# Diffusion trunk on one core: first Strassen pair of each phase reordered, ctx z written in float32 by ScalarE, six modulation rounds from TensorE to VectorE

## Chip, cores and metric

The kernel runs on one core of a Trainium2 chip. The metric is the device time of one execution in microseconds (us); lower is better. The engines are TensorE (PE, its weight loads PEld), VectorE (DVE), ScalarE (ACT), GpSimd (POOL) and SyncE (SP), whose queue issues most DMAs.

## The reference, cut to what matters

A trunk of two layers over 256 latent and 256 context (ctx) tokens of width 1024. Each layer is a modulated half-step SwiGLU, a token mixer (gMLP and attention in layer 0, mLSTM in layer 1) and a second half-step SwiGLU. The modulation vectors come from one matrix per layer, 1024 x 9216, times two vectors (one for latent tokens, one for ctx).

```python
def modulate(z, g, shift, scale):
    return rmsnorm(z, g) * (1 + scale) + shift

def swiglu(z, w13, w2):
    gate, up = jnp.split(z @ w13, 2, axis=-1)
    return (jax.nn.silu(gate) * up) @ w2
...
    for l in range(DEPTH):
        m_l = (s_lat @ mod_w[l] + mod_b[l]).reshape(b, N_MOD, 1, d)
        m_c = (s_ctx @ mod_w[l] + mod_b[l]).reshape(1, N_MOD, 1, d)
        h = h + 0.5 * m_l[:, 2] * swiglu(modulate(h, norm_g[l, 0], m_l[:, 0], m_l[:, 1]), ffn_w13[l, 0], ffn_w2[l, 0])
```

## The kernel before

**Precision.** Every float32 operand is split into a high part (ScalarE's copy to float32r) and a low part (VectorE's difference); `mm3` makes three matmuls, high by high, high by low and low by high. `wsplit` (L104 to L110) does it for weights: L108 the high part, L109 the low part, with four buffers of each (`NWH`). Raw weights lie in four slots of 1 MB (`rawp`), which DMAs on SP's queue fill.

**Phases.** `ffn512` runs three times over all 512 tokens: phase 1 (layer 0, first SwiGLU), phase 2 (layer 0, second) and phase 3 (layer 1, first). The last SwiGLU is another function. A phase has 11 column groups `cc` of 256 gate and 256 up columns. Most are a Strassen pair: gate and up by latent and ctx is a 2 x 2 block product done in seven products of half size, each 24 matmuls of 256 columns. Their operands on the token side are B11, B21, B22 (quarters of z) and T1 to T4 (sums of quarters, made once in a phase by `combos_lat`, `combos_ctx`, `combos_last` from z in float32); on the weight side a1, a2, g2 (plain weights), S1, S3 (sums that an accumulating DMA on POOL's queue makes in memory, L761), S2 = S3 + g2 and S4 = S2 + a2 (sums by VectorE, L776 and L778, written over a1's raw weights). `pair_products` runs the products in the order a1 B11, S2 T2, S1 T1, S3 T3, a2 B21, g2 T4, S4 B22 on three PSUM banks a, b, c; `pr.split` ahead of a product splits its weights, and `nx` is the next pair, whose loads (`Pair`, `plain`) are issued one pair ahead. The first column group of phases 2 and 3 is done directly, latent half first, then the ctx half, while the ctx half of z is still being normalised (`norm_z`: L408 VectorE, L411 ScalarE high part, L412 VectorE low part; its statistics go through a power on POOL, L125, and small pieces of it are queued in `pend` and run by `poke` between matmuls). Phase 1 does column groups 0, 1 and 2 directly, as six tiles of 128 gate and 128 up columns: three in the prologue, three here with `whole_tile`. After six column groups, and again after the other five, w2's products follow in columns `dp` with blocks of four.

**Modulation rounds.** A round is 512 columns of a modulation matrix; layer 0's rounds 0 to 3 are done in the prologue, the others in one of two ways. `mod_direct` does two rounds on TensorE: 32 matmul records (L310), a copy by ScalarE, four transposes and a sum by VectorE. `mod_round_dve` does one on VectorE: sixteen multiply-adds of 512 elements (L263, L265; eight from round 10 of layer 1 on, where the ctx vector isn't needed), which accumulate, and at its end four one-hot matmuls (L275, eight records) that set the sums into a PSUM bank shared by a group of rounds (`GROUPS`); the last of a group copies, transposes and adds the bias. It is a generator: `fill` runs one step of it, two multiply-adds, and `tick` calls `fill` at a rate per block of w2 (`FILL`); `mvec` runs what is missing where a vector is needed. Steps are given a priority 60 instructions ahead (`LEAD`). `until` is the last round that may be started.

**Order.** A scheduler at compile time orders each engine's instructions by priority (the order in the code) and readiness in its own model; on the chip each engine and each DMA queue runs its list in order.

## Time and profile before

| | before |
|---|---|
| three runs, median | 1736.99 us |
| three runs, lowest and highest | 1734.05, 1737.80 us |
| profiled execution | 1733.01 us |
| its span | 1731.3 us |
| granted TensorE clock over the span | 0.989 of 2.4 GHz |

The profile is of one execution. A table of stretches gives the busy time of each engine and the granted clock: 1.00 is 2.4 GHz, and a mean below it tells how much of the stretch ran at 1.2 GHz. In order of time, a row is start, duration, engine, line, operation, out<-in, and in brackets the idle time of the engine before it and what ended it. Matmuls overlap: a row's duration is longer than the distance to the next start, and the distance counts.

### The profile page before, as it was taken

Reading aid. Unit: us, or ns where it says so; the run is one execution under the profiler, and the core shown is the slowest. Engines: PE = TensorE matmul, PEld = TensorE weight load, DVE = VectorE, ACT = ScalarE, POOL = GpSimd, SP = SyncE. Lnnn points to the kernel's source line nnn. Section 1 sums busy time; section 2 is a strip of 40 time slices with the busy share of each in tenths; the row PEclk is TensorE's granted clock in tenths of the full one; section 3 lists DMA queues with packets and bytes.
Section 4 is the critical chain, followed back from the end, with each engine's and each line's share of the span. In section 5 each row is a group of like instructions: output and inputs, shape, how many; then the busy total and the mean of one; then the engine's idle time right before and its main releaser. Section 6 shows DMA issues by size and latency. Waiting matters only on the chain.

```text
span 1731.3 us, 30536 instructions
## 1 busy us (share of the span) xinstructions
PE 1687.0 (97%) x12247; PEld 1522.2 (88%) x12247; DVE 1259.1 (73%) x2067; ACT 739.2 (43%) x1140; POOL 287.7 (17%) x333
## 2 busy tenths in 40 slices
PE   7999999999999989999999899999999999999998
PEld 5799699989877989979998899779988788899998
DVE  5768668758665688967877888677876986695554
ACT  4443235424654355413542455214533554364443
POOL 0130133004432034013300241023200001100000
PEclk9999999999999989999999999999999999999999
DMA  9785787353466278468734586688555563146552
GB/s 282 211 179 183 215 219 175 106 163 110 150 226 147 66 176 186 158 184 206 172 108 159 132 204 153 232 224 202 121 191 153 188 226 122 50 130 211 189 180 71
DMA packets 274881, 292.63 MB, mean 169 GB/s; under 512 B 14648, under 2 KB 240948, under 8 KB 274740
## 3 DMA queue, kind: packets, MB, share of 16 engines
q1 hardware_dynamic: 242452, 261.31, 47.2%
q0 software_dynamic: 32256, 29.37, 11.8%
q8 instruction: 96, 1.57, 0.4%
q14 instruction: 45, 0.37, 0.1%
q10 hardware_dynamic: 32, 0.01, 0.0%
HBM read 289.60 MB, written 1.05 MB: 168 GB/s over the span
## 4 chain that ended last, share of the span: by engine, by line
PE 79%; issue 11%; DVE 7%; ACT 1%; SPq 1%; DMA 1%; POOL 1%; DVEq 0%; POOLq 0%; ACTq 0%
PE pb L789 14%; PE ps L114 11%; PE ps L116 11%; PE ps L115 11%; PE pc L789 9%; PE pa L789 9%; PE ps L1004 2%; PE ps L1006 2%; PE ps L1005 2%; PE mdir_ps L310 1%; DVE wlo L109 1%; PE mod_ps L275 1%; DVE zlo L412 1%; DVE nt L408 1%; PE pv_ps L1340 1%
## 5 line engine op out<-in xcount | busy, mean ns | idle before, releaser
L108 ACT CAST whi<-raw 128x1024 fp32r<-128x1024 f32 (+2 forms) x208 | 211.1, 1017 | 352.1 <-PE ps L115 183.4
L109 DVE TENSOR_TENSOR wlo<-raw,whi 128x1024 fp32r<-128x1024 f32 (+2 forms) x208 | 244.2, 1182 | 114.3 <-ACT whi L108 113.9
L761 POOL DMA_DIRECT2D rsum<-in_ffn_w_dram x224 | 197.8, 1037 | 607.3 <-DMA rsum<-in_ffn_w_dram 316.4
L114 PE MATMUL ps<-hh,whi 128*128 128x512 f32 (+1 forms) x764 | 270.5, 354 | 2.5 <-ACT whi L108 2.5
L116 PE MATMUL ps<-hh,wlo 128*128 128x512 f32 (+1 forms) x764 | 268.1, 351 | 1.7 <-DVE wlo L109 1.7
L115 PE MATMUL ps<-hl,whi 128*128 128x512 f32 (+1 forms) x764 | 268.5, 351 | 0.0
L114 PE MATMUL ps<-zhi,whi 128*128 128x256 f32 (+2 forms) x720 | 221.2, 310 | 3.1 <-ACT zhi L411 1.8
L116 PE MATMUL ps<-zhi,wlo 128*128 128x256 f32 (+2 forms) x720 | 219.6, 308 | 3.4 <-DVE wlo L109 3.3
L115 PE MATMUL ps<-zlo,whi 128*128 128x256 f32 (+2 forms) x720 | 219.8, 307 | 0.0
L108 ACT CAST whi<-rpl 128x1024 fp32r<-128x1024 f32 x112 | 117.7, 1051 | 186.2 <-DVE rpl L776 54.6
L109 DVE TENSOR_TENSOR wlo<-rpl,whi 128x1024 fp32r<-128x1024 f32 x112 | 136.8, 1222 | 71.4 <-ACT whi L108 71.2
L114 PEld LDWEIGHTS ps<-hh,whi 128*128 128x128 f32 x764 | 143.9, 188 | 30.1 <-issue 4.5
L116 PEld LDWEIGHTS ps<-hh,wlo 128*128 128x128 f32 x764 | 144.2, 189 | 25.5 <-DVE wlo L109 2.5
L115 PEld LDWEIGHTS ps<-hl,whi 128*128 128x128 f32 x764 | 144.0, 188 | 22.0 <-issue 1.6
L265 DVE SCALAR_TENSOR_TENSOR mod_acc<-raw,s_st,mod_acc 128x512 f32<-128x512 f32 x224 | 158.4, 744 | 4.8 <-DMA raw<-in_mod_w_dram 4.2
L114 PEld LDWEIGHTS ps<-zhi,whi 128*128 128x128 f32 x720 | 136.4, 190 | 14.9 <-issue 3.0
L116 PEld LDWEIGHTS ps<-zhi,wlo 128*128 128x128 f32 x720 | 135.9, 190 | 11.4 <-DVE wlo L109 4.4
L115 PEld LDWEIGHTS ps<-zlo,whi 128*128 128x128 f32 x720 | 136.5, 190 | 6.8 <-issue 1.0
L789 PE MATMUL pa<-zhi,wlo 128*128 128x256 f32 x448 | 128.6, 287 | 6.6 <-DVE wlo L109 6.6
L789 PE MATMUL pa<-zhi,whi 128*128 128x256 f32 x448 | 127.8, 285 | 1.7 <-ACT whi L108 1.7
L789 PE MATMUL pa<-zlo,whi 128*128 128x256 f32 x448 | 127.6, 285 | 0.0
L789 PE MATMUL pc<-zlo,whi 128*128 128x256 f32 x448 | 126.5, 282 | 0.0
(367 smaller groups left out, 4120.6 us busy)
## 6 DMA issues: line engine op xcount, KB each, us to landing
raw<-in_mod_w_dram SPq DMA_DIRECT2D x64, 1024.0 KB
raw<-in_ffn_w_dram SPq DMA_DIRECT2D x32, 1024.0 KB
raw<-in_ffn_w_dram SPq DMA_DIRECT2D x62, 512.0 KB
rsum<-in_ffn_w_dram SPq DMA_DIRECT2D x56, 512.0 KB
rsum<-in_ffn_w_dram POOLq DMA_DIRECT2D x224, 128.0 KB, 4.4
rpl<-in_ffn_w_dram SPq DMA_DIRECT2D x56, 512.0 KB
ra<-in_ffn_w_dram SPq DMA_DIRECT2D x28, 512.0 KB
raw<-in_ml_w_in_dram SPq DMA_DIRECT2D x12, 1024.0 KB
```

The lines of the kernel that those rows point to most:

```text
L108: act.copy(hi, view)
L109: dve.tensor_tensor(lo, view, hi.bitcast(F32), op=ALU.subtract)
L114: pe.matmul(ps, ah, bh, start=start, stop=False)
L115: pe.matmul(ps, ah, bl, start=False, stop=False)
L116: pe.matmul(ps, al, bh, start=False, stop=stop)
L265: dve.scalar_tensor_tensor(acc[:, v], raw[:, k], s1, acc[:, v], op0=ALU.mult, op1=ALU.add)
L275: pe.matmul(ps[32 * j : 32 * (j + 1), :256], onehot[:, MAXG - 1 - m : MAXG + 31 - m], acc[:, v, hf * 256 : (hf + 1) * 256], start=(m == 0) ...
L761: pool.dma_start(out=self.raw[n][:, k : k + 1], in_=src(cc, *two)[:, k : k + 1], accum_op=ALU.add)
L789: pe.matmul(o, a[:, k, cs], b[:, k], start=fresh and j == 0 and k == 0 and n == 0, stop=j == 1 and k == 3 and n == 2, skip_group_check=True,)
L1004: pe.matmul(o, zh, wh[:, k % 4], start=(k == 0), stop=False)
L1005: pe.matmul(o, zh, wl[:, k % 4], start=False, stop=False)
L1006: pe.matmul(o, zl, wh[:, k % 4], start=False, stop=(k == KD - 1))
```

## The change

- `ffn512` in phase 1: column group 2 is no longer two whole tiles but a pair, so a pair more and two 1 MB loads fewer.
- The first pair of each phase runs `pair_first`: order a1 B11, S4 B22, a2 B21, S2 T2, S1 T1, S3 T3, g2 T4, with S1 T1 on a fourth bank, d. The splits of a1, S2, S4 and a2 are all written ahead of it, and T1's.
- In phases 2 and 3 the first pair's loads (`Pair`) are written ahead of the direct tile, `combos` and `plain` between its latent and ctx half. ctx z in float32 is written by ScalarE in `norm_z` (eight operations of 256 elements) and not by two sums on VectorE.
- Modulation: layer 0's rounds 10, 11, 16, 17 and layer 1's 4 and 5 go from `mod_direct` to `mod_round_dve`. The even mixer has two `mod_direct` and not four, phase 3 has none, phase 1 keeps its one. The fill rates rise, a step is run after each pair, and in the odd mixer the first eight steps have no fill (`FILLODD`). In layer 0 the groups are (6, 12) and (16, 18), in layer 1 (4, 6) is new.

```diff
-FILL = ((1.9, 1.5), (1.9, 1.5), (1.9, 1.5))
-GROUPS = (((6, 10),), ((0, 4), (6, 10), (10, 12), (12, 16), (16, 18)))
+FILL = ((2.4, 2.1, 1), (2.4, 2.1, 1), (2.4, 2.1, 1))
+GROUPS = (((6, 12), (16, 18)), ((0, 4), (4, 6), (6, 10), (10, 12), (12, 16), (16, 18)))
-MIXDIRECT = {1: (10, 11), 4: (12, 13), 7: (14, 15), 10: (16, 17)}
+MIXDIRECT = {4: (12, 13), 8: (14, 15)}
+FILLODD = range(9, 33)
...
             act.activation(z[0][:, k, sl], t, AF.Identity, bias=B[:, k, half : half + 1])
+            if half == 1 and zctx[0] is not None:
+                act.activation(zctx[0][:, k], t, AF.Identity, bias=B[:, k, half : half + 1])
...
+            def pair_first(pr, nx, f):
+                a, b, c, d = bank("pa"), bank("pb"), abank("pc"), abank("pd")
+                w = pr.w
+                product(a, w["a1"], "B11", True)
+                s1 = sil_tile("s1")
+                act.copy(s1, a)
+                product(c, w["S4"], "B22", True)
+                product(a, w["a2"], "B21", False)
+                pr.split("S1")
+                product(b, w["S2"], "T2", True)
+                dve.tensor_tensor(s1, s1, b, op=ALU.add)
+                pr.split("S3")
+                product(d, w["S1"], "T1", True)
+                if nx:
+                    nx.plain()
+                pr.split("g2")
+                product(b, w["S3"], "T3", True)
+                s7 = sil_tile("s7")
+                dve.tensor_tensor(s7, s1, b, op=ALU.add)
+                dve.tensor_tensor(s7, s7, d, op=ALU.add)
+                act.activation(s7, s7, AF.Silu, scale=-1.0)
+                if nx:
+                    nx.split("a1")
+                product(b, w["g2"], "T4", False)
...
                 whole_tile(3, *first[1], 1)
-                combos_lat()
-                combos_ctx()
-                rg, ru = load_cc(2)
-                cc = 3
+                cc = 2
+                for n, ts in (("zlat", lat), ("zctx", ctx)):
+                    z_sum(z_tile(n), n, ts)
                 pr = Pair(cc)
-                for j in range(2):
-                    whole_tile(4 + j, rg, ru, j)
-                combos_last()
                 pr.plain()
-                pr.split("a1")
+                for n in ("a1", "S2"):
+                    pr.split(n)
+                combos()
+                split_to(mov["T1"], zf["zlat"][:, 0:4])
+                for n in ("S4", "a2"):
+                    pr.split(n)
             else:
...
                 cc = 1
+                z_sum(z_tile("zlat"), "zlat", lat)
+                zctx[0] = z_tile("zctx")
+                pr = Pair(cc)
                 for n, ts in enumerate((lat, ctx)):
...
-                    if n == 0:
-                        combos_lat()
-                    else:
+                    if n == 1:
                         settle()
-                        combos_ctx()
-                        pr = Pair(cc)
+                        zctx[0] = None
+                        combos()
+                        pr.plain()
...
-                combos_last()
-                pr.plain()
-                pr.split("a1")
+                for n in ("a1", "S2", "S4", "a2"):
+                    pr.split(n)
+                split_to(mov["T1"], zf["zlat"][:, 0:4])
...
-                    pair_products(pr, nx, cc * 2 - f0)
+                    (pair_first if ahead.pop() else pair_products)(pr, nx, cc * 2 - f0)
+                    ahead.append(False)
+                    tick(rates[2])
...
-                fill(1)
+                ran[0] += 1
+                if ran[0] in FILLODD:
+                    fill(1)
...
-    filler.extend([(0, r) for r in range(6, 10)] + [(1, r) for r in range(18) if r not in (4, 5)])
+    filler.extend([(0, r) for r in range(6, 12)] + [(0, 16), (0, 17)] + [(1, r) for r in range(18)])
...
-    ffn512(1, 0, z, nxt, FILL[2], direct=(4, 5))
+    ffn512(1, 0, z, nxt, FILL[2])
```

## Rows read from the trace of the kernel before

**Rows 1.** The page, busy us, share of the span and instructions of each engine.

```profile
PE 1687.0 (97%) x12247; PEld 1522.2 (88%) x12247; DVE 1259.1 (73%) x2067; ACT 739.2 (43%) x1140; POOL 287.7 (17%) x333
```

**Rows 2.** Stretches: start:end, length, busy us (instructions) per engine, granted clock, DMA.

```profile
612.00:641.00 29.00, 24.40 (x169) 23.40 (x168) 24.26 (x25) 15.07 (x18) 9.65 (x12) 0.82 0.72 164
...
641.00:732.00 91.00, 91.00 (x759) 90.37 (x758) 78.43 (x94) 46.21 (x55) 20.68 (x24) 1.00 0.70 180
...
980.00:1014.00 34.00, 28.26 (x214) 27.55 (x213) 29.04 (x29) 16.78 (x20) 10.58 (x12) 0.90 0.77 189
...
1109.00:1130.00 21.00, 18.33 (x96) 11.91 (x95) 13.14 (x22) 4.79 (x5) 0.00 (x0) 0.92 0.71 233
...
1354.00:1376.00 22.00, 18.33 (x71) 13.33 (x71) 21.61 (x45) 9.01 (x11) 0.00 (x0) 0.92 0.38 125
```

**Rows 3.** TensorE in order of time, even mixer: start, us, engine, line, operation.

```profile
458.74 3.64 PE L310 MATMUL mdir_ps<-raw,s_st 128*32 128x512 f32 x32
...
463.11 0.66 PE L119 MATMUL mdirT_ps<-ident,mdir_sb 128*128 128x128 f32 x4
```

**Rows 4.** TensorE in order of time, phase 3's direct rounds.

```profile
1111.05 3.64 PE L310 MATMUL mdir_ps<-raw,s_st 128*32 128x512 f32 x32
...
1117.63 0.50 PE L114 MATMUL ps<-hh,whi 128*128 128x512 f32 x1 [1.55 <-ACT whi L108]
```

**Rows 5.** Groups of instructions by line: busy us, mean ns | idle before, releaser.

```profile
L265 DVE SCALAR_TENSOR_TENSOR mod_acc<-raw,s_st,mod_acc 128x512 f32<-128x512 f32 x224 | 158.4, 744 | 4.8 <-DMA raw<-in_mod_w_dram 4.2
...
L108 ACT CAST whi<-rpl 128x1024 fp32r<-128x1024 f32 x112 | 117.7, 1051 | 186.2 <-DVE rpl L776 54.6 <-PE pc L789 47.4 <-PE pb L789 46.3
...
L109 DVE TENSOR_TENSOR wlo<-rpl,whi 128x1024 fp32r<-128x1024 f32 x112 | 136.8, 1222 | 71.4 <-ACT whi L108 71.2
...
L825 DVE TENSOR_TENSOR s<-s,pb 128x512 f32<-128x512 f32 x28 | 19.2, 686 | 14.6 <-PE pb L789 14.6
```

**Rows 6.** TensorE in order of time, one-hot matmuls together and spread.

```profile
337.40 0.64 PE L275 MATMUL mod_ps<-mod_acc,onehot 128*32 128x256 f32 x8
337.97 0.50 PE L114 MATMUL ps<-hh,whi 128*128 128x512 f32 x1
...
767.67 0.39 PE L116 MATMUL ps<-hh,wlo 128*128 128x512 f32 x1
767.99 0.62 PE L275 MATMUL mod_ps<-mod_acc,onehot 128*32 128x256 f32 x2
...
771.79 0.40 PE L115 MATMUL ps<-hl,whi 128*128 128x512 f32 x1
```

**Rows 7.** SP queue, TensorE and VectorE in order of time, start of phase 1.

```profile
61.44 1.74 SPq L97 DMA_DIRECT2D raw<-in_ffn_w_dram  x2
...
66.95 0.50 PE L114 MATMUL ps<-zhi,whi 128*128 128x512 f32 x1 [0.74 <-ACT sil L847]
...
72.96 0.92 SPq L759 DMA_DIRECT2D rsum<-in_ffn_w_dram  x2
...
88.82 1.23 DVE L776 TENSOR_TENSOR rpl<-rsum,rpl 128x1024 f32<-128x1024 f32 x1 [2.73 <-DMA rsum<-in_ffn_w_dram]
```

**Rows 8.** Chain that ended last, in order of time: start, us, what.

```profile
100.64 2.88 PE pa L789 x24
...
120.50 2.88 PE pa L789 x24
```

**Rows 9.** TensorE in order of time, first product of phase 2.

```profile
623.59 0.39 PE L789 MATMUL pa<-zhi,wlo 128*128 128x256 f32 x1 [2.27 <-DVE wlo L109]
```

**Rows 10.** TensorE in order of time, odd mixer.

```profile
1358.28 0.50 PE L116 MATMUL ps<-zhi,wlo 128*128 128x512 f32 x1 [1.99 <-DVE wlo L109]
...
1371.61 0.50 PE L116 MATMUL ps<-zhi,wlo 128*128 128x512 f32 x1 [1.31 <-DVE wlo L109]
```

**Rows 11.** POOL in order of time, start of phase 2.

```profile
602.94 0.70 POOL L125 TENSOR_TENSOR rs<-rs,mhalf 128x2 f32<-128x2 f32 x1 [17.21 <-DMA rsum<-in_ffn_w_dram]
...
609.70 2.66 POOL L761 DMA_DIRECT2D rsum<-in_ffn_w_dram  x3 [2.61 <-issue]
```

More of the change, by code (lines that the diff above doesn't have):

```diff
@@ L419, in norm_z @@
             )
+    zctx = [None]
     def norm_A(A, l, i, ks):
@@ L662, in ffn @@
                         elif half == 0 and k0 == 0:
-                            while current[0] is not None or (until[0] == (0, 17) and filler and filler[0] <= until[0]):
+                            while current[0] is not None or (until[0] == (0, 11) and filler and filler[0] <= until[0]):
                                 fill(1, more=False)
@@ L842, in pair_products @@
                 store(f, 2, s7, ctx)
+            def pair_first(pr, nx, f):
[22 more added lines that the diff above has]
+                product(b, w["g2"], "T4", False)
+                s2 = sil_tile("s2")
+                dve.tensor_tensor(s2, s1, c, op=ALU.add)
+                dve.tensor_tensor(s2, s2, d, op=ALU.add)
+                dve.tensor_tensor(s7, s7, s2, op=ALU.mult)
+                store(f, 2, s7, ctx)
+                dve.tensor_tensor(s1, s1, b, op=ALU.add)
+                act.activation(s1, s1, AF.Silu, scale=-1.0)
+                dve.tensor_tensor(s1, s1, a, op=ALU.mult)
+                store(f, 2, s1, lat)
             def hidden(f, pg, pu):
@@ L896, in ffn512 @@
                         mm3(pss[a][:, ts], ws[a][0][:, k], ws[a][1][:, k], z[0][:, k, ts], z[1][:, k, ts], k == 0, k == KD - 1)
[L897 to L899 removed]
+                for n in ("a1", "S2", "S4", "a2"):
+                    pr.split(n)
+                split_to(mov["T1"], zf["zlat"][:, 0:4])
                 for j in range(2):
                     hidden(j, pss[2 * j], pss[2 * j + 1])
+            ahead = [True]
             gate = tmp.tile([P, KD, 2], F32, tag="gate", name="gate")
@@ L953, in ffn512 @@
                             elif half == 0 and k0 == 0:
-                                while current[0] is not None or (until[0] == (0, 17) and filler and filler[0] <= until[0]):
+                                while current[0] is not None or (until[0] == (0, 11) and filler and filler[0] <= until[0]):
                                     fill(1, more=False)
@@ L1727, in odd_mixer @@
         g = kvo()
+        ran = [0]
         def run(n):
```

25 lines of the change are left out of this document (10 added, 15 removed).

## The prediction

> **What bounds the kernel now.** I read the busy table first [rows 1]: TensorE is busy 1687.0 of 1731.3 us, VectorE 1259.1, so time is won where TensorE's instructions become fewer or where it stands still. The table of stretches [rows 2] then shows where the missing 44 us and the slow clock are. In the pairs of a phase (641 to 732) nothing is lost. At the start of phase 2 (612 to 641) TensorE is idle 4.6 us and the granted clock is 0.82, so the 1.2 GHz level held for 0.36 of 29 us; counted in matmuls, 169 at the 0.120 us that 641 to 732 gives (91.0 / 759) are 20.3 us, so 8.7 us are lost. At the start of phase 3 (980 to 1014) 214 matmuls are 25.7 of 34 us: 8.3 lost. Around the direct rounds of phase 3 (1109 to 1130) it idles 2.7 us, and at clock 0.92 about 3.4 us run at half rate, which costs 1.7. At the start of the odd mixer (1354 to 1376) 3.7 us idle and 1.8 of clock are lost. In the even mixer the direct rounds cost only their own TensorE time.
>
> **The sum's base.** The profiled execution took 1733.0 us (span 1731.3); the median of the three runs is 1737.0, 4.0 more. I add the terms to the first and move the result to the median.
>
> **Direct rounds removed.** In the even mixer a pair of rounds is 32 records in 3.64 us and four transposes in 0.66 [rows 3]; the tail of each group overlaps what follows, so 3.6 and 0.4 are taken from the products. Two of four such pairs go: **-8.0**. Their eight 1 MB loads leave SP's queue there and appear in the feed-forward phases. In phase 3 the removed pair takes 3.6 us (1111.05 on), the next product starts only at 1117.63 after a wait of 1.55 on ScalarE [rows 4]; with the 2.7 idle and 1.7 of clock of that stretch and 0.3 of transposes it is **-8.2**. Between -4 (its own time alone) and -9.
>
> **The same six rounds on VectorE.** Each is 16 operations at 744 ns [rows 5], 11.9 us, 71 in all. They lie in stretches where VectorE has room: 78.4 of 91 us in the pairs [rows 2]. But TensorE isn't rid of them: each round ends in four one-hot matmuls (eight records). Where they stand together they take 0.6 to 0.7 us (337.40 to 337.97); where the compiled order has them one by one between the 512-column matmuls, 767.67 to 771.79 holds four one-hot steps and five ordinary matmuls, 4.12 less 5 x 0.234, 2.95 us [rows 6]. The twelve rounds of this size now stand in both forms and in one with two pieces; I take 1.5 each, near the mean of the ten that can be read, and 0.5 for two more group ends: **+9.5**, between 4 and 18. So about three fifths of what the direct rounds cost come back.
>
> **Phase 1's two whole tiles become a pair.** From 66.95 [rows 7], after a wait of 0.74, to 100.64 [rows 8] three whole tiles run in 33.7 us, so two take 22.5, each 48 matmuls of 0.234; a pair of seven products runs from 100.64 to 120.50, 19.9 us [rows 8]: -2.6. But the cover goes as well. The pair's first product needs a1, the second S4 = (S3 + g2) + a2. S3 is summed in memory: base load issued at 72.96, the add that uses it starts at 88.82, 15.9 us later [rows 7]. The new pair's base can't start before tile 3's weights leave their slot, when now the next weights start, 61.44 [rows 7]; so S3 is there at 77.3. Behind it is a serial chain, since every sum is written over the weights that the step before it still reads: add 1.22, S2 high 1.05, S2 low 1.22, add 1.22, S4 high 1.05 and low 1.22 [rows 5, 7], 7.0 us, to 84.3. TensorE ends tile 3 at 78.2 and a1's product at 81.0: 2.9 us wait (the high part lets it start a little before). Between 0 and 6.
>
> **A new wait in every first pair.** In the new order T3's and T4's products stand next to each other on bank b; T4's adds onto what T3's left, and between them VectorE must read b. Today another product stands there and hides it. The read takes 0.69 us and starts behind a wait on TensorE in nearly all pairs (14.6 us over 28) [rows 5]: 0.8 us three times if VectorE is free, 2 each if it isn't. Phase 1: -2.6 + 2.9 + 0.8 = **+1.1**.
>
> **First pairs of phases 2 and 3.** Removed: two VectorE sums of 1.2 us for ctx z (ScalarE writes it now, eight operations that run beside), and products that need T2 and T1 come fourth and fifth. Added ahead: S2, S4 and a2 splits, queued on VectorE behind the combinations. Today the a1 product waits 2.27 us for its low part [rows 9]. Laid out with the rows' durations, a1's low part is there at about 620 in phase 2, as the direct tile ends; VectorE still has two further splits and the end of the combinations in its queue, and the chain of 7 us above ends near 628.5, where a1's product ends at 623. So TensorE stands 5.4 us before the second product instead of in three pieces before and in the first two. All later operands are then ready. With the bank's 0.8 the loss is 6.3 at full clock, and 1.6 more at 1.2 GHz: 7.9 against 8.7 and the 0.6 of smaller waits around, 9.3. In phase 3 the same layout gives 9.8 against 8.3 and 1.5 of waits up to the second pair: nothing won. **-1.4** for both. Bounds: a1's slot frees 4.3 us before the direct tile ends, so with VectorE free the chain would end 2.2 us late, and -7 each; with T4 and the hidden tiles served first, +3 each.
>
> The half rate stands in the rows where TensorE was busy 24.4 of 29 us, and a wait of the size of today's keeps its cost in my layout [rows 2]. The Trainium skill, "TensorE: Matmul & The Clock Gate", section on the HAM clock gate, makes half rate the default that activity releases, and lists it for an idle engine; read that way a first pair with scattered waits would keep 2.4 GHz, and phases 2 and 3 would end about 3.4 us earlier, the sum at 1725.6. That lies inside the forecast's own spread, and as the trace disagrees it has no chance of its own.
>
> **Odd mixer.** The first eight steps no longer carry a fill, so two 1 MB loads leave SP's queue ahead of a projection weight and 16 operations leave VectorE. The wait of 1.31 at 1371.61 goes, of the 1.99 at 1358.28 [rows 10] only the 0.4 of one operation, perhaps the half rate with it: **-2.5**, between 0 and -5.
>
> **Crowding.** A fill per pair is 1.5 us of VectorE in 19.9, from 86% to 93%, takes one of four weight slots for four pairs, and sets a 1 MB load on SP's queue ahead of pair loads. At phase 2's gate four steps are forced at once under 16 us of the next column's matmuls. 29 pairs at 0 to 0.5: I take **+1.5**, up to 14.
>
> Sum: -8.0 - 8.2 + 9.5 + 1.1 - 1.4 - 2.5 + 1.5 = -8.0: 1725.0 for the profiled execution, **1729** for the median.
>
> **The rivals.** *First pairs come out smooth* (1716): VectorE serves a1, S2 and S4 ahead of the T splits; each of the three phases then loses only the bank's 0.8 and one or two us. For it: the products that need no combination are 8.5 us of cover. Against: the serial chain. *The one-hot steps are all spread* (1737): six at 2.9 instead of 1.5, +8.4; for it, the new rounds end inside columns and pairs, where the spread form stands today. This is no change. *Slower, by the POOL queue* (1745): the first pair's loads are now written ahead of the statistics of the ctx half. Today POOL does the power at 602.94 and the adds behind it, the fourth at 609.70 [rows 11]. If the order puts S3's four adds first, the power comes 7.7 us later, and with it the whole normalisation on which VectorE's chain in phases 2 and 3 hangs: +6 and 2 of clock, twice. It decides as soon as the power stands behind the third add; against it, the power was ready before the base load had landed in both phases. *Slower, by crowding* (1742): half a us in each of 26 pairs. That the change does not do what it says has no place: the products, rounds and loads it names must move.
>
> **How the numbers follow.** Forecast 0.43 (1724 to 1733), smooth 0.18, spread 0.20, POOL 0.11, crowding 0.08. About 0.2%, 3.5 us, is what a measurement of this kernel can tell from no change. Faster: the forecast but for its upper edge, and smooth, 0.62. Within: the spread case and the edge, 0.21. Slower: 0.17. The range goes from the smooth case to just below POOL's, 1714 to 1743.
>
> **What would show it.** Right: two L310 groups in the even mixer, none in phase 3, and no wait there; one wait of 4 to 6 us before the second product of phases 2 and 3 and about 3 in phase 1, released by the split of S4; a wait near 0.8 before T4's product, released by VectorE's read of b; 26 one-hot rounds where 20 stand, with a mean near 1.5 us for the big ones. Wrong: no wait before S4's product; a wait in the pairs on late low parts; the direct tile of the ctx half waiting for its statistics.

## The result, and the profile of the changed kernel

The changed kernel took 1750.7 us (median of four runs, 1750.2 to 1752.7) against 1736.7 of the kernel before: a ratio of 1.0085, 95% interval 1.0068 to 1.0103. It is **slower by 14 us**, where 8 us less were forecast, and the time lies outside the range. The profiled execution took 1750.24 us, its span 1748.5.

The page of the changed kernel: busy time by engine [rows 1], the chain that ended last, and the group of VectorE's modulation steps [rows 5].

```profile
PE 1695.5 (97%) x12263; PEld 1522.9 (87%) x12263; DVE 1321.5 (76%) x2170; ACT 745.8 (43%) x1159; POOL 294.9 (17%) x341
...
PE 71%; issue 12%; DVE 10%; DMA 4%; ACT 1%; SPq 1%; POOL 1%; DVEq 0%; POOLq 0%; ACTq 0%
...
L266 DVE SCALAR_TENSOR_TENSOR mod_acc<-raw,s_st,mod_acc 128x512 f32<-128x512 f32 x308 | 217.1, 746 | 24.1 <-DMA raw<-in_mod_w_dram 23.4
```

TensorE is busy 8.5 us longer although six rounds left it. VectorE's idle time ahead of these multiply-adds has grown from 4.8 us [rows 5] to 24.1, nearly all of it until a raw load landed. The stretches (columns as in [rows 2]): the even mixer, the first pair of phase 2, its first w2 columns, the first pair of phase 3, its first w2 columns.

```profile
410.40:601.30 190.90, 186.73 (x1506) 162.94 (x1505) 130.44 (x328) 103.85 (x231) 63.12 (x68) 1.00 0.32 99
626.90:661.00 34.10, 30.98 (x251) 29.96 (x252) 30.40 (x37) 17.01 (x21) 14.11 (x16) 1.00 0.87 213
733.10:812.50 79.40, 75.47 (x318) 56.24 (x315) 62.76 (x98) 15.14 (x17) 8.64 (x11) 0.96 0.63 195
1002.90:1037.00 34.10, 27.55 (x197) 26.28 (x196) 27.27 (x31) 14.44 (x18) 13.16 (x15) 0.90 0.78 190
1113.90:1190.20 76.30, 75.75 (x319) 55.60 (x315) 58.91 (x89) 14.04 (x15) 9.73 (x11) 1.00 0.69 207
```

To see where the time went I cut both traces into stages, each from its first matmul on TensorE to the first of the next. "One-hot" is the part of a stage that the one-hot matmuls take: from the matmul ahead of a group to the one behind it, less 0.2335 us for each 512-column and 0.1187 us for each 256-column matmul between. The last four columns are kernels of the next section: the modulation part (e3_mod) and the pair part (e4_pair) of the change alone, and the whole change and the pair part with the one-hot matmuls together (e5_same, e7_pair_same).

| us (of it one-hot) | before | changed | e3_mod | e4_pair | e5_same | e7_pair_same |
|---|---|---|---|---|---|---|
| up to phase 1 | 20.9 | 23.1 | 20.8 | 21.1 | 22.5 | 23.4 |
| phase 1: direct tiles, first chunk's pairs | 139.1 | 142.1 | 144.1 | 141.5 | 149.3 | 143.6 |
| first w2 columns | 78.0 (4.4) | 81.6 (5.7) | 85.1 (7.2) | 78.0 (4.7) | 78.1 (2.0) | 75.8 (2.4) |
| second chunk's pairs | 99.9 (0.7) | 103.0 (3.5) | 102.4 (2.9) | 99.9 (0.7) | 100.2 (0.7) | 99.2 |
| second w2 columns | 58.5 (0.7) | 60.6 (2.9) | 63.4 (5.7) | 58.4 (0.7) | 59.4 (1.3) | 59.1 (1.3) |
| even mixer | 199.0 | 190.9 | 191.0 | 200.1 | 190.4 | 199.5 |
| phase 2: direct tile, first chunk's pairs | 133.1 | 131.7 (0.7) | 132.2 (0.7) | 127.7 | 129.5 | 127.8 |
| first w2 columns | 71.6 (4.2) | 79.4 (10.1) | 74.5 (6.6) | 71.7 (4.2) | 75.3 (6.3) | 68.7 (1.3) |
| second chunk's pairs | 99.9 (0.7) | 102.4 (2.9) | 102.4 (2.9) | 99.9 (0.7) | 100.0 (0.7) | 99.3 |
| second w2 columns | 59.9 (2.0) | 63.1 (4.9) | 63.1 (4.9) | 59.9 (2.0) | 60.2 (2.0) | 60.0 (2.0) |
| phase 3: direct tile, first chunk's pairs | 134.1 | 135.9 (0.7) | 136.2 (0.7) | 131.0 | 135.1 | 131.0 |
| first w2 columns | 79.6 (3.8) | 76.3 (8.4) | 77.3 (9.4) | 78.0 (3.8) | 74.4 (3.3) | 75.8 (1.6) |
| second chunk's pairs | 99.9 (0.7) | 101.5 (2.0) | 101.5 (2.0) | 99.9 (0.7) | 99.9 (0.6) | 99.2 |
| second w2 columns | 60.4 (1.9) | 62.4 (3.3) | 62.7 (3.6) | 60.4 (1.9) | 64.4 (4.0) | 61.0 (2.6) |
| odd mixer to the end | 391.4 (3.6) | 387.8 (2.2) | 387.4 (2.2) | 391.0 (3.6) | 387.1 (1.9) | 391.3 (3.7) |
| one-hot in all | 22.7 | 47.3 | 48.7 | 23.0 | 22.7 | 14.8 |

The mixer gains what was forecast. The one-hot matmuls cost 24.6 us more, and they cost more in nearly every stage, also where no round was added. This is one round in the form in which half of the two-vector rounds stand in the changed kernel, in TensorE's order of time (pairs of phase 1):

```profile
260.98 0.28 PE L789 MATMUL pa<-zhi,wlo 128*128 128x256 f32 x1
261.19 0.62 PE L276 MATMUL mod_ps<-mod_acc,onehot 128*32 128x256 f32 x2
261.74 0.39 PE L789 MATMUL pb<-T4h,whi 128*128 128x256 f32 x1
262.06 0.62 PE L276 MATMUL mod_ps<-mod_acc,onehot 128*32 128x256 f32 x2
...
263.79 0.62 PE L276 MATMUL mod_ps<-mod_acc,onehot 128*32 128x256 f32 x2
264.34 0.39 PE L789 MATMUL pb<-T4h,whi 128*128 128x256 f32 x1
```

Four one-hot steps and four products take 3.36 us from 260.98 to 264.34; less 4 x 0.1187 that is 2.89, as in the spread form of before [rows 6]. Of the 18 rounds with two vectors, 9 stand in three or four pieces like this in the changed kernel, 4 in two pieces and 5 together; before, of 12, it was 3, 2 and 7. Of the eight with one vector, 3 are in two pieces (1.38 us) where all eight were together (0.65). Counted round by round (they run in the order of the filler's list), the six new rounds take 12.8 us, 3.9 of it one wait that is shown below; the other twenty take 34.3, where they took 22.7 before.

The second thing to see is VectorE, then TensorE, in phase 3's first pair:

```profile
1027.10 0.88 DVE L264 TENSOR_SCALAR mod_acc<-raw,s_st 128x512 f32<-128x512 f32 x2 [2.63 <-DMA raw<-in_mod_w_dram]
1027.90 0.74 DVE L266 SCALAR_TENSOR_TENSOR mod_acc<-raw,s_st,mod_acc 128x512 f32<-128x512 f32 x1
1028.56 1.22 DVE L110 TENSOR_TENSOR wlo<-rpl,whi 128x1024 fp32r<-128x1024 f32 x1
1029.70 0.68 DVE L863 TENSOR_TENSOR s<-s,pb 128x512 f32<-128x512 f32 x1
...
1030.43 0.39 PE L789 MATMUL pb<-T4h,whi 128*128 128x256 f32 x1 [2.67 <-DVE s L863]
```

VectorE stands 2.63 us before a modulation step whose raw load has not landed; the read of bank b (L863), for which TensorE's next product T4 waits, is queued behind it, after two more operations. TensorE's waits for these sums s are 8.1 us in five places, 0.8 in one before. The third is the gate of phase 2, where rounds 16 and 17, no longer in the mixer, are due:

```profile
741.76 8.04 DVE L266 SCALAR_TENSOR_TENSOR mod_acc<-raw,s_st,mod_acc 128x512 f32<-128x512 f32 x12
...
749.18 1.07 PE L276 MATMUL mod_ps<-mod_acc,onehot 128*32 128x256 f32 x4 [3.93 <-DVE mod_acc L266]
```

```profile
748.00:753.00 5.00, 3.82 (x12) 1.57 (x13) 3.81 (x6) 1.22 (x2) 0.00 (x0) 0.50 0.37 124
```

Twelve multiply-adds run without a break, TensorE waits 3.93 us for the last, and the one-hot matmuls behind it take 1.07 us for a piece, at a granted clock of 0.50.

### The profile page after: what moved, and what is told of

The parts are those of the page before. It is cut to its first block, busy times and chain, and to the rows that moved or that the text cites. A ratio compares the mean times of both kernels' runs of the same rounds, so it can differ in the third digit from the quotient of the medians.

```text
span 1748.5 us, 30674 instructions
## 1 busy us (share of the span) xinstructions
PE 1695.5 (97%) x12263; PEld 1522.9 (87%) x12263; DVE 1321.5 (76%) x2170; ACT 745.8 (43%) x1159; POOL 294.9 (17%) x341
## 4 chain that ended last, share of the span: by engine, by line
PE 71%; issue 12%; DVE 10%; DMA 4%; ACT 1%; SPq 1%; POOL 1%; DVEq 0%; POOLq 0%; ACTq 0%
PE pb L789 12%; PE ps L115 10%; PE ps L116 9%; PE ps L117 9%; PE pc L789 8%; PE pa L789 7%; DVE wlo L110 3%; DMA raw<-in_mod_w_dram 3%; PE mod_ps L276 2%; PE ps L1045 2%; PE ps L1046 2%; PE ps L1047 2%; DVE mod_acc L266 1%; DVE zlo L415 1%; DVE nt L409 1%
## 5 line engine op out<-in xcount | busy, mean ns | idle before, releaser
L110 DVE TENSOR_TENSOR wlo<-raw,whi 128x1024 fp32r<-128x1024 f32 (+2 forms) x204 | 239.3, 1181 | 111.7 <-ACT whi L109 111.1
L761 POOL DMA_DIRECT2D rsum<-in_ffn_w_dram x232 | 205.2, 1035 | 628.2 <-DVE wlo L110 169.0
L266 DVE SCALAR_TENSOR_TENSOR mod_acc<-raw,s_st,mod_acc 128x512 f32<-128x512 f32 x308 | 217.1, 746 | 24.1 <-DMA raw<-in_mod_w_dram 23.4
L115 PE MATMUL ps<-zhi,whi 128*128 128x256 f32 (+2 forms) x688 | 207.1, 304 | 2.8 <-ACT zhi L412 1.8
L117 PE MATMUL ps<-zhi,wlo 128*128 128x256 f32 (+2 forms) x688 | 206.3, 303 | 1.7 <-DVE wlo L110 1.7
L116 PE MATMUL ps<-zlo,whi 128*128 128x256 f32 (+2 forms) x688 | 206.7, 302 | 0.0
L117 PEld LDWEIGHTS ps<-hh,wlo 128*128 128x128 f32 x764 | 144.1, 189 | 26.3 <-issue 4.5
L115 PEld LDWEIGHTS ps<-zhi,whi 128*128 128x128 f32 x688 | 129.8, 189 | 11.0 <-ACT zhi L412 2.2
L117 PEld LDWEIGHTS ps<-zhi,wlo 128*128 128x128 f32 x688 | 129.8, 190 | 7.4 <-DVE wlo L110 2.2
L116 PEld LDWEIGHTS ps<-zlo,whi 128*128 128x128 f32 x688 | 130.1, 189 | 5.0 <-issue 0.4
L789 PE MATMUL pc<-zhi,whi 128*128 128x256 f32 x440 | 123.9, 281 | 2.3 <-ACT whi L109 2.3
```

What stands on the lines that cost most here:

```text
L110: dve.tensor_tensor(lo, view, hi.bitcast(F32), op=ALU.subtract)
L115: pe.matmul(ps, ah, bh, start=start, stop=False)
L116: pe.matmul(ps, ah, bl, start=False, stop=False)
L117: pe.matmul(ps, al, bh, start=False, stop=stop)
L266: dve.scalar_tensor_tensor(acc[:, v], raw[:, k], s1, acc[:, v], op0=ALU.mult, op1=ALU.add)
L761: pool.dma_start(out=self.raw[n][:, k : k + 1], in_=src(cc, *two)[:, k : k + 1], accum_op=ALU.add)
```

## The experiments

Two theories stood at first: *the one-hot matmuls stand spread* (TensorE's own time), and *crowding* (VectorE's added steps and their raw loads). A rival to both was that *the new first pairs* cost the time. Every run was compared with the kernel before, 1735.0 to 1735.5 us in these comparisons. Each edit also makes the compiled order of other instructions anew; the stages show how far that goes.

**e1_together, e2_before_together.** The edit, on the changed kernel and on the one before:

```diff
+        edge = acc.rearrange("p v (h c) -> p v h c", h=2)[:, :, :, 0:1]
+        dve.tensor_copy(edge, edge)
+        with tc.high_priority(offset=1000):
             for j in range(2 * nv):
```

> The changed kernel with the one-hot matmuls of each round held together: a one-element VectorE copy per quarter of mod_acc makes the four quarters come ready at once, and the four matmuls get a higher priority, so that no product matmul stands between them (26 groups of TensorE instructions in the order in place of 59). VectorE's rounds, the raw loads and the first pairs stay as they are. Theory 'one-hot matmuls spread' (a round whose quarters stand singly between product matmuls holds TensorE 2.86 to 2.89 us, one whose quarters stand together 0.65; in the changed kernel's trace the groups sum to 47 us, 4 of it a wait): 26 x 0.65 = 17 us, so 25 to 30 us less, 1721 to 1725. Rival 'crowding' (the loss is in VectorE's queue and the raw loads, which this leaves): 1745 to 1750. Rival 'first pairs' (the new order of products costs it): also 1745 to 1750.

> The kernel before with the same edit and nothing else: the control for the edit. In its trace the one-hot matmuls sum to about 20 us in 20 rounds, in 31 groups; with the edit 26 groups stand in the order. Theory 'one-hot matmuls spread': 3 to 6 us less, 1731 to 1734, so that the order of the two kernels turns over when both have it. Rivals 'crowding' and 'first pairs': no change here (1735 to 1738), and no turn-over.

Measured: 1747.6 (1.0070, 1.0050 to 1.0091) and 1740.4 (1.0022, 1.0010 to 1.0035): 3 us less and 5 us more. Both missed what the theory of spread matmuls gave, and the first lies in the range of the two rivals. The matmuls do stand together, but the high priority puts them ahead of the time at which VectorE is done (TensorE, e1_together):

```profile
240.59 0.64 PE L279 MATMUL mod_ps<-mod_acc,onehot 128*32 128x256 f32 x8 [1.51 <-DVE mod_acc L275]
241.16 0.50 PE L115 MATMUL ps<-hh,whi 128*128 128x512 f32 x1
```

The edit swapped spreading for waits (32.5 us of one-hot matmuls in place of 47.3, of it 14.5 of waits before 11 of the 26 rounds, 0.6 to 2.1 us each), so it settled nothing; it does show that the eight records take 0.64 us together in the changed kernel too.

**e3_mod, e4_pair.** The change in two: the lists GROUPS, MIXDIRECT, FILL, FILLODD, the filler's list, the step behind each pair and no direct rounds in phase 3, on the kernel before; and pair_first, ctx z and phase 1's pair, without those.

```diff
 e3_mod:
                     pair_products(pr, nx, cc * 2 - f0)
+                    tick(rates[2])
 e4_pair:
                     (pair_first if ahead.pop() else pair_products)(pr, nx, cc * 2 - f0)
                     ahead.append(False)
-                    tick(rates[2])
```

> The kernel before with the modulation part of the change alone: two direct rounds and two single ones out of the mixer and two out of the start of phase 3, their rounds on VectorE, a fill step after every pair, the new rates and the new odd list; first pairs, ctx z and phase 1's whole tiles as before. Theory 'one-hot matmuls spread' (64 groups stand in its order, at 0.72 us each 46 us against 20 before, +26; a wait of some 4 us for a forced round; mixer -8.2 as the stage table showed, phase 3 about -8): 1748 to 1752. Rival 'first pairs': the modulation part alone comes out as predicted for it, -8.0 - 8.2 + 9.5 + 1.5 = -5.2, 1731. Rival 'crowding': slower too, about 1745, but with the loss in pairs and columns where no one-hot matmul stands.

> The kernel before with the rest of the change alone: the first pair of each phase in the new order with four banks, ctx z in float32 from ScalarE, phase 1's two whole tiles as a pair; modulation as before. Theory 'one-hot matmuls spread': the predicted sum of these terms, +1.1 - 1.4 = -0.3, up to +5 with the bank waits of 1.1 to 2.7 us that the changed kernel's trace shows before T4: 1736 to 1741. Rival 'first pairs': the whole loss, 1745 to 1751. Rival 'crowding': 1734 to 1738.

Measured: 1752.8 (1.0102, 1.0080 to 1.0124) and 1728.4 (0.9963, 0.9948 to 0.9978). The rival *first pairs* falls: by themselves they are 7 us faster, and faster than any of the three forecasts for e4_pair. The whole loss, and more, is in the modulation part (+17 us; 48.7 us of one-hot matmuls). The two parts sum to +10, together they are +14: the first pairs of phases 2 and 3 take 127.7 and 131.0 us alone and 131.7 and 135.9 in the changed kernel. TensorE's waits for the sums s are 3.9 us in e3_mod, in eight places, and 8.1 in the changed kernel: they don't need the new order of products, but it has more of them.

**e5_same, e6_before_same, e7_pair_same.** A second way to hold a round's matmuls together. Every instruction has a priority by its place in the program; the fill moves its own 60 places forward, so that the four one-hot matmuls have four successive numbers, which product matmuls have as well. Here all four get one:

```diff
         for j in range(2 * nv):
             v, hf = j // 2, j % 2
+            with tc.high_priority(offset=-20 + j):
                 pe.matmul(
```

> The changed kernel; the four one-hot matmuls of a round share one place in the order of priorities (with numbers of their own they alternated with product matmuls that had the same numbers), so that 28 groups stand in TensorE's order in place of 59, without being hurried as in e1_together, whose groups stood together but whose trace shows TensorE waiting 1 to 2 us for mod_acc before 12 of its 26 rounds (32.5 us in all). Theory 'one-hot matmuls spread, at a price of 0.65 a group': 28 x 0.65 = 18 us against 47, and the forced round of phase 2 keeps its wait of 4: 25 us less, 1725; with waits before a third of them as in the run before, 1735. Rival 'crowding' (VectorE's steps and raw loads hurt the first pairs and columns themselves): 1742 to 1750.

> The kernel before with the same edit: 20 groups in place of 31, so 13 us against 22.7. Theory 'spread': -9, 1727. Rival 'crowding': no change, 1736.

> The pair part alone (1728.4 when it was timed) with the same edit. Theory 'spread': -9, 1719 to 1720, faster than either kernel. Rival 'crowding': 1728.

Measured: 1736.4 (1.0011, 0.9993 to 1.0029), 1725.8 (0.9949, 0.9935 to 0.9964), 1721.7 (0.9926, 0.9911 to 0.9941): 14.4, 9.6 and 6.7 us less than the same kernels without the edit. For the kernel before -9 was expected, for the changed one 1725, or 1735 if waits came in place of the spread. One round in e5_same, TensorE:

```profile
266.24 0.28 PE L790 MATMUL pb<-T4h,whi 128*128 128x256 f32 x1
266.44 0.64 PE L277 MATMUL mod_ps<-mod_acc,onehot 128*32 128x256 f32 x8
267.01 0.39 PE L790 MATMUL pb<-T4l,whi 128*128 128x256 f32 x1
```

0.77 us from matmul to matmul, 0.65 more than without it. In e5_same the one-hot matmuls fall by 24.6 us, yet the time by 14.4 only. Most of what was given back (7 us) is in phase 1's first chunk: it stands in VectorE and TensorE ahead of T4 in the first pair, and in the row of the stretch 81.2 to 171.9:

```profile
105.54 0.88 DVE L264 TENSOR_SCALAR mod_acc<-raw,s_st 128x512 f32<-128x512 f32 x2 [4.54 <-DMA raw<-in_mod_w_dram]
...
108.14 0.68 DVE L864 TENSOR_TENSOR s<-s,pb 128x512 f32<-128x512 f32 x1
...
108.87 0.58 PE L790 MATMUL pb<-T4h,whi 128*128 128x256 f32 x1 [4.53 <-DVE s L864]
```

```profile
81.20:171.90 90.70, 84.09 (x674) 83.48 (x673) 75.77 (x89) 41.71 (x49) 22.12 (x25) 0.94 0.69 173
```

A raw load lands 4.54 us late, T4's product waits 4.53 us, and the stretch has a granted clock of 0.94. Like against like, the loss has become smaller but is not gone: e5_same is 10.6 us slower than e6_before_same, where the changed kernel is 14.1 slower than the one before. From e7_pair_same to e5_same, that is for the modulation part with matmuls together, it is 14.6 us, 7.9 of it one-hot matmuls (14.8 and 22.7).

**e8_no_first_tick.** No fill step behind the first pair of a phase:

```diff
+                    if not lead:
                         tick(rates[2])
```

> As e5_same, without the fill step behind the first pair of each phase (three steps fewer; the bursts at the gates make them up). First pairs took 106.2, 111.0 us in phases 2 and 3 of the changed kernel and 102.5, 106.1 us with the pair part alone, 0.6 us apart in phase 1. Theory 'VectorE's fill steps delay what frees the bank ahead of T4': 4 to 9 us less than e5_same. Rival 'the steps there come from earlier columns and raw loads': within 2 us of e5_same.

Measured: 1730.2 (0.9966, 0.9948 to 0.9985), 6.1 less than e5_same, as expected; but the stages say it is not the whole of the first theory. Phase 1's first stage falls from 149.3 to 143.7 us, those of phases 2 and 3 don't (129.7 and 136.1, against 129.5 and 135.1), and in all three phases a wait ahead of T4 now stands in the second pair, 2.07, 1.60 and 3.35 us. VectorE in phase 3:

```profile
1029.13 0.49 DVE L264 TENSOR_SCALAR mod_acc<-raw,s_st 128x512 f32<-128x512 f32 x1 [4.80 <-DMA raw<-in_mod_w_dram]
...
1031.72 0.68 DVE L826 TENSOR_TENSOR s<-s,pb 128x512 f32<-128x512 f32 x1
```

The wait follows the fill step, in the second pair's older order of products too.

**e9_no_raw, e14_pair_no_raw, e15_after_no_raw, e16_before_no_raw.** VectorE's rounds read a constant in place of their loads, in four kernels:

```diff
-            raw = wraw(mod_w[l], 4 * kh, 4, r * 512, 512)
+            flat = small.unsqueeze(1).to_broadcast([P, 4, P])
```

> As e5_same, but the raw loads of VectorE's modulation rounds are left out and its steps read a constant tile, so that the modulation values are not the reference's; the number and length of VectorE's steps and of the one-hot matmuls stay. In e5_same VectorE stood 30.4 us in 12 places before mod_acc until a raw load landed, and TensorE 10.4 us for the sums s behind it, ahead of T4, and 2.0 us for mod_acc. Theory 'a step that waits for its raw load holds VectorE's queue': 10 to 14 us less, 1722 to 1726. Rival 'VectorE's added time itself': 1733 to 1737, with the waits for s as they were.

> As e7_pair_same without the raw loads of VectorE's rounds (its steps read a constant tile, so that the modulation values are not the reference's): the control for e9_no_raw, which ran 20 us faster than e5_same. Theory 'a step that waits for its raw load holds VectorE's queue ahead of the sums s' (in e7 VectorE stands 11.9 us in 9 places, TensorE 0.2 us for mod_acc and never for s): 0 to 4 us less, 1718 to 1722, so that the 14.6 us between e5_same and e7 turn into -2 to -6. Rival 'the traffic of the raw loads itself': 15 us less or more, 1705.

> The changed kernel without the raw loads of VectorE's rounds (constant tile in their place, modulation values not the reference's), its one-hot matmuls still spread (61 groups). If spread groups and raw loads cost each by itself: 20 us less as in e5_same, 1730. If the waits were a consequence of the spread: under 10 us less, above 1740.

> The kernel before without the raw loads of VectorE's rounds (constant tile in their place, modulation values not the reference's). VectorE stands 7.6 us in 8 places for them, TensorE 0.8 us for s. Theory 'waits in VectorE's queue': 0 to 4 us less, 1731 to 1735, while the same cut takes 20 us from the changed kernel's design. Rival 'traffic': 12 us less or more, 1723.

Measured: 1716.0 (0.9891, 0.9875 to 0.9906), 1728.3 (0.9961, 0.9947 to 0.9976), 1741.3 (1.0034, 1.0022 to 1.0045) and 1735.4 (1.0004, 0.9992 to 1.0016). The first fell by more than was expected, the second missed and is slower, the third came out as for waits that follow from the spread, the fourth as for waits in VectorE's queue.

| us | matmuls as they stood | matmuls together | together, no raw loads | as they stood, no raw loads |
|---|---|---|---|---|
| before | 1735.5 | 1725.8 | - | 1735.4 |
| pair part | 1728.4 | 1721.7 | 1728.3 | - |
| whole change | 1750.7 | 1736.4 | 1716.0 | 1741.3 |

The rival *traffic* finds no support. From the kernel before this takes 40 loads of 1 MB (289.60 MB read by its page, 247.66 by that of e16_before_no_raw), and its time is the same; from the pair part with matmuls together it takes as many, and that is slower. From the changed kernel the same cut takes 9.4 us, and 20.4 from e5_same, in the stages where VectorE stood for a load: phase 1's first chunk -8.0, phase 2's first columns -4.1, phase 3's first chunk and columns -2.9 and -3.9; TensorE waits 1.0 us for s, 10.4 before (its waits in e5_same, then in e9_no_raw):

```profile
PE pb L790 <- DVE s L864: 7.2, 3, 4.5
...
PE pb L790 <- DVE s L826: 3.2, 2, 2.4
```

```profile
PE pb L793 <- DVE s L867: 1.0, 1, 1.0
```

In e15_after_no_raw it waits neither for s nor at the gate of phase 2, so that the 3.93 us there are in what is saved. VectorE's steps are all still there, so their number alone does not cost this. The edit also frees the weight slots that the raw loads took and makes the order anew: the runs price the loads as a whole, and that it is the wait in VectorE's queue is read from the rows. That both cuts together give 34.7 and not 14.4 + 9.4 fits the waits that e5_same shows in place of the spread matmuls, but isn't shown by a run. One more wait is in no account here. A round's first operation overwrites the one accumulator `mod_acc`, and VectorE's queue stands there until the one-hot matmuls of the round before have read it. The changed kernel, then e15_after_no_raw:

```profile
L264 DVE TENSOR_SCALAR mod_acc<-raw,s_st 128x512 f32<-128x512 f32 x44 | 19.8, 483 | 41.9 <-PE mod_ps L276 31.7 <-DMA raw<-in_mod_w_dram 10.2
```

```profile
L267 DVE TENSOR_SCALAR mod_acc<-small,s_st 128x512 f32<-128x512 f32 x44 | 20.0, 486 | 43.8 <-PE mod_ps L279 42.7 <-PE pa L117 1.1
```

These 31.7 us are 16.0 in the kernel before and 11.7 in e5_same; with the loads left out they are 42.7 with the matmuls spread and 16.7 with them together. A second accumulator, which would price this, was not tried. One result I can't explain: e14_pair_no_raw is 6.6 us slower than e7_pair_same, 4.1 of it in the first pairs of phase 2, where the operands of the first products come later (waits of 1.01, 1.62 and 0.76 for low and high parts).

**e10_keep_16_17, e11_keep_4_5.** Some of the moved rounds direct again, on e5_same:

```diff
 e10_keep_16_17:
-MIXDIRECT = {4: (12, 13), 8: (14, 15)}
+MIXDIRECT = {4: (12, 13), 7: (14, 15), 10: (16, 17)}
 e11_keep_4_5:
-    ffn512(1, 0, z, nxt, FILL[2])
+    ffn512(1, 0, z, nxt, FILL[2], direct=(4, 5))
```

> As e5_same with layer 0's rounds 16 and 17 back in the mixer as direct rounds, which are due again in phase 2. Phase 2's first chunk of w2 columns took 75.3 us in e5_same and 68.7 us with the pair part and the same one-hot edit; a direct pair in the mixer is worth 4.2 us by the stage table (-8.4 for two). Theory 'the gate of phase 2 forces these two rounds': -6.6 + 4.2, 2 to 4 us less, 1732 to 1734. Rival 'the loss there belongs to layer 1's rounds and the rates': 1740.

> As e5_same with layer 1's rounds 4 and 5 back on TensorE as direct rounds at phase 3's gate. The prediction had 8.2 us for them there and 3.2 us for two rounds on VectorE: 1741 by that. By the stages the whole of phase 3 from its first pair on took 348.9 us in e5_same and 342.1 us with the pair part and the same one-hot edit, although two direct rounds stand in the latter: 3 to 6 us less, 1730 to 1733, if these two rounds are what the phase pays for.

Measured: 1735.8 (0.9999, 0.9986 to 1.0011) and 1740.3 (1.0023, 1.0002 to 1.0044). The first lies between its two forecasts and within the noise of e5_same, so it is inconclusive: the mixer is 5.4 us longer, phase 2's first columns 74.1 in place of 75.3; their rounds are then layer 1's, brought forward. The second missed: with the direct rounds back the kernel is 4 us slower by the medians, where 3 to 6 less were expected; the intervals overlap, so the 4 us are not clear of noise. Nothing here says that moving those two costs time, and the medians come near the 5 us (8.2 - 3.2) that the prediction's terms gave for it.

**e12_move_10_11, e13_move_rates.** On e7_pair_same, one direct pair of the mixer on VectorE, at the old rates and at higher ones:

```diff
-MIXDIRECT = {1: (10, 11), 4: (12, 13), 7: (14, 15), 10: (16, 17)}
+MIXDIRECT = {4: (12, 13), 7: (14, 15), 10: (16, 17)}
 e13_move_rates:
-FILL = ((1.9, 1.5), (1.9, 1.5), (1.9, 1.5))
+FILL = ((2.4, 2.1), (1.9, 1.5), (1.9, 1.5))
```

> The pair part with the one-hot edit (e7, 1721.7) and one direct pair of the mixer, rounds 10 and 11 of layer 0, on VectorE in phase 1, whose columns have room for six rounds at the old rates; no fill step behind pairs, phases 2 and 3 as in e7. Theory 'rounds on VectorE are cheap where their one-hot matmuls stand together and no step is forced or put behind a pair': -4.2 + 2 x 0.65 + 0.5 for the group, 1719. Rival 'each round moved to VectorE costs more than it saves': 1723 to 1727.

> As e12_move_10_11 with phase 1's fill rates raised from 1.9 and 1.5 to the changed kernel's 2.4 and 2.1. In e12_move_10_11 (1732.6 against 1721.7 of e7) the stages are as in e7 but for the mixer (-3.7) and phase 1's last w2 columns (+12.2: one-hot matmuls 10.5 us, 5.2 of it a wait for mod_acc, TensorE's clock at 0.93), where the two rounds that the columns had not reached are issued in one go ahead of the mixer. Theory 'the burst at the gate': 11 to 13 us less than e12_move_10_11, 1719 to 1722. Rival 'each round on VectorE costs more than it saves, wherever it runs': 1727 to 1732.

Measured: 1732.6 (0.9981, 0.9969 to 0.9994) and 1721.7 (0.9926, 0.9910 to 0.9941). The first missed, and its list of waits on TensorE names the place:

```profile
PE mod_ps L276 <- DVE mod_acc L265: 5.4, 2, 5.2
```

One wait of 5.2 us at the end of phase 1, where the rounds that are due before the mixer are issued in one go. With rates that bring them in earlier these 11 us are gone, as forecast. Of the 4.1 us that the mixer gains, 2.8 go into phase 1's columns, 77.6 and 60.1 us where e7_pair_same has 75.8 and 59.1; by the medians the move is worth nothing.

**e17_mixer_rounds, e18_four_rounds.** On e13_move_rates: all the mixer rounds that the change moved, or phase 3's two, with fill steps only behind pairs of second chunks:

```diff
+                    if ch:
+                        tick(rates[2])
 e17_mixer_rounds:
+FILL = ((2.6, 2.3, 3), (1.9, 1.5, 0), (1.9, 1.5, 0))
 e18_four_rounds:
+FILL = ((2.4, 2.1, 1), (2.2, 1.8, 1), (2.2, 1.8, 1))
```

> As e13_move_rates, with rounds 16 and 17 of layer 0 too on VectorE in phase 1, as in the changed kernel's mixer, but not left for phase 2's gate: phase 1's rates 2.6 and 2.3 and three fill steps behind each pair of its second chunk, none behind a pair of a first chunk. Theory 'a moved round pays where its matmuls stand together, no gate forces it and no step stands behind a pair of the first chunk': mixer -4.2, two rounds of 0.65: 1718 to 1719. Rival 'steps behind pairs cost wherever they stand' (phase 1 has 15): 1724 or more.

> As e13_move_rates, with layer 1's rounds 4 and 5 on VectorE as in the change: rates 2.2 and 1.8 in phases 2 and 3, one fill step behind each pair of the second chunks only. From e5_same against e11_keep_4_5 (-3.9): 1717 to 1719. By the prediction's term (-8.2 for the direct rounds, +0.65 for each round that stands together, +0.5 for the group): 1715. Rival 'steps behind pairs cost wherever they stand': 1723 or more.

Measured: 1732.8 (0.9984, 0.9974 to 0.9994) and 1719.4 (0.9895, 0.9871 to 0.9919). e17 missed, and by its time it lies with the rival. But its 15 steps behind pairs do not show the loss: the second chunk of pairs, where they stand, takes 100.8 us, 1.5 more than in e13_move_rates, 1.3 of it one-hot matmuls, and TensorE waits 0.9 us for s in all (in e18 one such wait, 2.65 us behind a raw load that was 4.35 us out, brings the chunk to 102.9). Phase 1's columns grow by 5.3 and 8.8 us against e13_move_rates, and its first chunk by 5.9: the first pair (81.18 to 101) has a granted clock of 0.83 and waits of 1.81 and 1.89 (1.00, 0.20 and 1.89 in e13_move_rates). e18 has the same there (0.82), though neither of the two runs a step behind it. The second chunk of pairs of e17_mixer_rounds, then TensorE's wait behind it, then the second chunk of e7_pair_same:

```profile
250.40:351.20 100.80, 100.80 (x858) 99.72 (x857) 93.56 (x116) 47.85 (x58) 25.08 (x29) 1.00 0.72 184
```

```profile
359.63 0.80 PE L116 MATMUL ps<-hh,wlo 128*128 128x512 f32 x1 [5.09 <-DVE wlo L109]
```

```profile
242.80:342.10 99.30, 99.30 (x842) 99.26 (x841) 76.89 (x86) 49.86 (x59) 24.65 (x28) 1.00 0.65 158
```

VectorE is busy 93.6 of 100.8 us there (76.9 of 99.3 in e7_pair_same) and comes to the next columns' low parts late. At these rates phase 1 has no room for eight rounds. e18 came out just above what was expected. Of the kernels that compute everything it has the lowest median, 16 us below the one before; its 2 us below e13_move_rates are within the noise.

e18 and e10_keep_16_17 together say what no run was made for. Both have the same four rounds on VectorE, the new first pairs and the matmuls together; they differ in the rates of phases 2 and 3, in the step behind pairs of first chunks and in FILLODD alone. They are 16.3 us apart (1719.4 and 1735.8). TensorE waits 8.6 us for s and 5.4 for `mod_acc` in e10_keep_16_17, 2.7 and 0.2 in e18; phases 2 and 3 together take 641.4 us in the first and 617.4 in the second, and the odd mixer gives 8.5 of that back. So the pace of the fill costs here, and not that these rounds are on VectorE. Which part of the pace it is, no run tells.

## Why the prediction was wrong, point by point

**Direct rounds removed, -8.0 and -8.2: right.** The mixer takes 190.9 us, 199.0 before: -8.1. Phase 3's first w2 columns, without their one-hot matmuls, go from 75.8 to 67.9: -7.9.

**The six rounds on VectorE, +9.5: this is the step that failed.** All one-hot matmuls went from 22.7 to 47.3 us, +24.6. The prices of the forms were right (2.9 spread, 0.65 together), and so was the sum for the six themselves: 8.9 us without the wait at the gate. What failed is that I left the other twenty alone: they went from 22.7 to 34.3. The mean of the eighteen big rounds is 2.2 us and not 1.5. The form is set by where a fill step falls among the products; e5_same and e6_before_same show that the numbers of the priorities decide it. The places of the old rounds moved with the new rates, the steps behind pairs and the longer list (no run takes these three apart), and rounds that had stood together were torn apart. The rival "all spread" had the mechanism, at +8.4 for the six; but of the six only one stands in four pieces, and the twenty were missing from it. Another 3.93 us of the 24.6 is the wait at phase 2's gate; the prediction named the forced steps and set them at nothing.

**Crowding, +1.5: failed too.** TensorE's waits for VectorE's sums went from 0.8 to 8.1 us. The step that I counted as 1.5 us of VectorE's time holds its queue as long as the raw load is out (2.63, 4.54 and 4.80 us in the rows above), and what is behind it is just the read that the new order had put on the path (in the old order, e3_mod, the waits are 3.9). I had both halves, the load on SP's queue and the bank's read, and did not put one behind the other. Leaving the loads out with the matmuls as they stood gives 9.4 us (e15_after_no_raw), the wait at the gate among them.

**Phase 1's pair, +1.1: measured +3.0** (139.1 to 142.1), +2.4 with the pair part alone. The wait before T4 was 1.08. The wait for S4 was there too, but 1.89 and not the 2.9 laid out, since a part of T2's product was put ahead:

```profile
86.92 0.38 PE L789 MATMUL pc<-zhi,whi 128*128 128x256 f32 x1 [1.89 <-ACT whi L109]
```

**First pairs of phases 2 and 3, -1.4: measured -8.5 alone and -1.0 in the change** (without the one-hot matmuls that stand there now). The one long wait of 5.4 us before the second product did not come: TensorE's order took T2's product first, and phase 2's first pair of the changed kernel runs at a granted clock of 1.00 with waits of 0.73, 0.39, 0.44 and 1.49 where it had 0.82 [rows 2]. Alone (e4_pair) this is the case that I called smooth; with the fill, T4's waits took it back (1.49 and 1.56 in phase 2, 2.67 in phase 3). That -1.0 came out so near to -1.4 is luck: two errors of 7 us cancel. On the clock, the Trainium skill, "TensorE: Matmul & The Clock Gate", section on the HAM clock gate, has half rate as the default, which activity releases. I read that as full rate in a pair with scattered waits and gave it no chance; phase 2 came out so (1.00), phase 3 did not (0.90, waits of 2.65 and 2.67).

**Odd mixer, -2.5: -2.2** without its one-hot matmuls (387.8 to 385.6).

These terms come to +8.4 of the 16.5 us by which the stages differ (-8.1 - 7.9 + 24.6 + 3.0 - 1.0 - 2.2); the waits for the sums are spread over their stages. Of the rest, 2.3 and 1.9 are in the first w2 columns of phases 1 and 2, 1.7 in the second chunks; 2.2 lie ahead of phase 1, where untouched code took 20.8 to 23.4 us in these traces, so that they say nothing of the change.

**The other rivals.** In phase 2 POOL did the power at 608.61, ahead of S3's adds at 610.48, and in phase 3 at 987.99, ahead of the adds at 988.78: that rival did not happen.

```profile
608.61 0.70 POOL L126 TENSOR_TENSOR rs<-rs,mhalf 128x2 f32<-128x2 f32 x1 [17.38 <-DVE rs L125]
610.48 2.75 POOL L761 DMA_DIRECT2D rsum<-in_ffn_w_dram  x3 [1.18 <-DMA rsum<-in_ffn_w_dram]
```

Two slips of the prediction's own sums change nothing of this: the terms named for phase 3's direct rounds add to 8.3 and not 8.2, and the chance of "faster" (0.62) is more than its two cases have (0.43 and 0.18).

By the stages the forecast of -8.0 became +16.5. Of these 24.5 us, 15.1 are the one-hot matmuls, 6.6 are left for crowding (8.1 against 1.5, and 2.2 of it lie ahead of phase 1), 1.9 are phase 1's pair and 0.9 the rest. That is where the time stands in the traces, not what each cause is worth by itself: with the matmuls together in both kernels the loss is still 10.6 us, and only with the raw loads left out as well does the whole change (1716.0, with that work left out) fall below the kernel before with matmuls together (1725.8). Both causes are shown, and that the waits hang on the pace of the fill (e18 and e10_keep_16_17); how the 14 us divide between the two is not. What stays open besides is why the raw loads cost 20 us with the matmuls together and 9 without, and why e14_pair_no_raw is slower than its base.

## What to carry to other kernels

Work that is scattered between other work has a price for each place in which it stands: when a rate or a list changes, count again all of its places, not only the added ones, and look in the compiled order whether pieces that belong together still do. Before a step that waits for a load is put into an in-order queue, read what stands behind it there; if the pacing engine waits for that, the load's lateness is on the path. A gate that forces unfinished work is priced as the whole of that work, unless the steps up to it are counted and suffice.

## What the runs showed of the hardware

A one-hot matmul with 32 output columns holds TensorE about 0.55 us when it stands alone (261.19 to 261.74), and four of them that use the four quarters of the array run in 0.57 us in all (266.44 to 267.01): side by side they overlap, with a full matmul between them they don't. Taking 40 MB of loads away from a kernel whose TensorE hardly waits behind them (0.8 us) changed its time by nothing measurable (1735.4 against 1735.0); with as many left out, another kernel became 6.6 us slower (1728.3 against 1721.7), for which no run has the reason.
